# Four S pairs instead of three in each group of the MLP's first product, with the blocks loaded by diagonals

## The chip, the cores and the metric

The kernel runs on one core of a Trainium2 chip. The metric is the device time of one execution, in microseconds (us). Five engines work side by side: TensorE (PE; its weight loads are listed as PEld), VectorE (DVE), ScalarE (ACT), GpSimd (POOL) and SyncE (SP), whose queue issues the loads of weights.

## The reference

A decoder block: attention and a state-space mixer side by side, merged, and then the MLP that this case is about. x has 256 rows of 2048, w_up is 2048 x 8192 and w_down 8192 x 2048, all float32.

```python
merged = sigmoid(gate_att) * (att @ w_att_branch) + sigmoid(gate_ssm) * (y @ w_ssm_branch)
x = x + merged @ w_out
h2 = rms_norm(x, norm2_g)
x = x + square(relu(h2 @ w_up)) @ w_down
```

## The kernel before

Every large product is made in three parts. A float32 weight tile `raw` is copied to a rounded tile `hi` on ScalarE (`split`, L111), and VectorE makes the rest `lo = raw - hi` (L112). The other operand is split in the same way, and TensorE adds hi x hi, hi x lo and lo x hi into one bank of PSUM. Buffers: four `raw` tiles (`RAW`), three `hi` and three `lo`, each of 128 x 1024; a load waits until its `raw` buffer has been read out, a split until TensorE has given a `hi` buffer back.

The MLP goes in two halves of the hidden layer (`for h in range(2)`: `up(h)`, then `down(h)`). `up` has four groups for each half; a group makes 1024 columns of the product for both tiles of 128 rows, over 16 k tiles taken as eight pairs. `down` has two such groups for each half, over 16 pairs each. `mixed` runs a group; the letter of each pair in `UP` or `DOWN` says how its 2 x 2 x 2 block product (two row tiles, two k tiles, two column blocks of 512) is made:

- N and P: eight block products, 24 matmuls of 128x512. The weights are the two `raw` tiles of 1024 columns, each split whole (`pieces_n`).
- S: seven block products of sums of blocks (Strassen's way in Winograd's form), 21 matmuls. `pieces_s` makes the four sums of weight blocks on VectorE: `t13` holds the first and third, `t24` the second and fourth; h1/l1, a hi/lo buffer, h3/l3 and h4/l4 are the splits. h1, l1, t13, t24, h4 and l4 have one buffer each.

The left operands of `up` are made ahead by `norm_task` and `left`, those of `down` by `u_operands` and `left` (L863 to L883), as far as the scheduler moves them forward into the groups of `up`.

A group has seven banks, q1 to q7 in the numbering of `product`. At its end `combine` adds them on VectorE (ScalarE copies q1 first, L1025): `u2 = q6 + q1` and `u3 = q7 + u2` (both L1016), then q2, q5, q3 and q4 with them. Only S pairs write q1, q6 and q7, so these are complete after the last S pair; N pairs write q2, q5, q3 and q4. A next group's product takes a bank as it is given back by `combine`. `u_task` then transposes the results on TensorE (L1073), 16 transposes a group.

The order on each engine is fixed at compile time by a scheduler that lists instructions by the times of its own model; each engine's queue then runs strictly in that order.

Of the kernel before, what the change touches and what calls it, by code (L numbers as in the profile page):

```python
# [32 lines left out]
HD = 128  # L33
IH = 16

UP = "NSNSNSNN"
DOWN = ('NNSNNPPSPPPPSPPP', 'PPSPPPPSPPPPSPPP')
NB = 32
TOPK = 64
# [8 lines left out]
def body(tc, x, x_t, vectors, taps, w_in, dt_bias, a_log, d_skip, bias_t, w_att_branch,  # L48
# [10 lines left out]
    with ctx:  # L59
# [48 lines left out]
        def split(raw, shape):  # L108
            hi = wpool.tile(shape, F32R, name=nm("hi"), tag="hi", bufs=3)
            lo = wpool.tile(shape, F32R, name=nm("lo"), tag="lo", bufs=3)  # L110
            a.copy(hi, raw)  # L111
            v.tensor_tensor(lo, raw, hi.bitcast(F32), op=OP.subtract)  # L112
            return hi, lo
# [831 lines left out]
        def pieces_s(w, kk, c0):  # L945


            r0, r1 = (load(w, kk + i, 1, c0, 1024)[:, 0] for i in range(2))
            h1 = fp.tile([P, 512], F32R, name=nm("h1"), tag="h1", bufs=1)
            l1 = fp.tile([P, 512], F32R, name=nm("l1"), tag="l1", bufs=1)  # L950
            a.copy(h1, r0[:, :512])
            v.tensor_tensor(l1, r0[:, :512], h1.bitcast(F32), op=OP.subtract)
            h2, l2 = (z[:, 0] for z in split(r1, [P, 1, 1024]))
            t13 = fp.tile([P, 2, 512], F32, name=nm("t13"), tag="t13", bufs=1)
            v.tensor_tensor(t13[:, 0], r0[:, :512], r0[:, 512:], op=OP.add)
            v.tensor_tensor(t13[:, 1], r0[:, 512:], r1[:, 512:], op=OP.add)
            h3, l3 = split(t13, [P, 2, 512])
            t24 = fp.tile([P, 2, 512], F32, name=nm("t24"), tag="t24", bufs=1)
            v.tensor_tensor(t24[:, 0], t13[:, 0], r1[:, 512:], op=OP.add)
            v.tensor_tensor(t24[:, 1], t24[:, 0], r1[:, :512], op=OP.add)  # L960
            h4 = fp.tile([P, 2, 512], F32R, name=nm("h4"), tag="h4", bufs=1)
            l4 = fp.tile([P, 2, 512], F32R, name=nm("l4"), tag="l4", bufs=1)
            a.copy(h4, t24)
            v.tensor_tensor(l4, t24, h4.bitcast(F32), op=OP.subtract)
            return {1: (h1, l1), 2: (h2[:, :512], l2[:, :512]), 3: (h2[:, 512:], l2[:, 512:]),
                    5: (h3[:, 0], l3[:, 0]), 7: (h3[:, 1], l3[:, 1]),
                    6: (h4[:, 0], l4[:, 0]), 4: (h4[:, 1], l4[:, 1])}

# [197 lines left out]
```

## Time and profile before

| | us |
|---|---|
| median of 3 runs | 1979.37 (1977.62 to 1980.09) |
| the profiled execution | 1978.39 |
| its span in the trace | 1976.3 |
| PE busy in the span | 1963.7 (99%) |
| DVE busy | 1500.6 (76%) |
| ACT busy | 1063.6 (54%) |

The first product runs from about 1280 to 1458 (first half) and from 1630 to 1802 (second half). A busy time is the union of the instructions' durations; matmuls and VectorE's operations overlap their neighbours, so the cost of one in a row of many is read from start to start. The granted clock of TensorE is 1.0 of full speed in all the stretches below.

### The profile page before, as it was taken

To read this page: it belongs to the slowest core of one execution; us is meant where nothing else is said; L and a number is where in the kernel's file an instruction comes from. 1 tells how busy PE (TensorE), PEld (TensorE's weight loads), DVE (VectorE), ACT (ScalarE), POOL (GpSimd) and SP (SyncE) were. 2 spreads that over 40 slices of the span, in tenths; PEclk is the share of its full clock that TensorE was granted. 3 is DMA by queue.
4 is the path that set the end of the run, shared out by engine and by line. 5 is a ranking of instruction groups with operands and counts; after the bars stand their busy time and mean duration, and the time that the engine had idled before them with its cause. 6 is when DMAs were issued, how large, how long until landed. Compare 5 with 4: busy or idle time off the path is not lost.

```text
span 1976.3 us, 26219 instructions
## 1 busy us (share of the span) xinstructions
PE 1963.7 (99%) x9437; PEld 1633.8 (83%) x9437; DVE 1500.6 (76%) x2465; ACT 1063.6 (54%) x1562; POOL 38.2 (2%) x93
## 2 busy tenths in 40 slices
PE   9999999999999999999999999999999999999998
PEld 7878888888888888888888888788888888888887
DVE  7868656558888887888656556699878888887886
ACT  6555545444455554545544544566665555665554
POOL 2000000000000000000000000000000000000000
PEclk9999999999999999999999999999999999999999
DMA  7646555476666566565566666555565665656664
GB/s 229 211 134 185 182 166 167 160 222 187 181 186 186 181 187 187 176 186 173 171 197 186 193 193 229 174 192 191 193 198 187 211 200 186 204 186 195 193 222 149
DMA packets 132226, 372.25 MB, mean 188 GB/s; under 512 B 18288, under 2 KB 18928, under 8 KB 131840
## 3 DMA queue, kind: packets, MB, share of 16 engines
q1 hardware_dynamic: 128704, 357.87, 58.1%
q0 software_dynamic: 3248, 12.65, 1.9%
q8 instruction: 74, 1.21, 0.2%
q14 instruction: 56, 0.46, 0.1%
q10 hardware_dynamic: 144, 0.06, 0.0%
HBM read 368.37 MB, written 2.16 MB: 187 GB/s over the span
## 4 chain that ended last, share of the span: by engine, by line
PE 98%; DVE 1%; ACT 1%; DMA 0%; issue 0%; SPq 0%; DVEq 0%; ACTq 0%
PE mb L153 42%; PE mb L981 31%; PE mb L127 10%; PE mb L128 5%; PE ab L981 3%; PE ab L748 1%; PE ab L1073 1%; PE ab L458 1%; PE ab L692 0%; PE ab L767 0%; PE ab L740 0%; PE ab L712 0%; DMA raw<-in_w_in_dram 0%; PE ab L552 0%; PE ab L577 0%; PE ab L573 0%
## 5 line engine op out<-in xcount | busy, mean ns | idle before, releaser
L112 DVE TENSOR_TENSOR lo<-raw,hi 128x1024 fp32r<-128x1024 f32 x628 | 765.5, 1222 | 361.1 <-ACT hi L111 359.3
L111 ACT CAST hi<-raw 128x1024 fp32r<-128x1024 f32 x628 | 658.1, 1052 | 619.5 <-PE mb L153 329.1
L153 PE MATMUL mb<-hi,h_hl 128*128 128x512 f32 x1408 | 444.2, 393 | 0.0
L153 PEld LDWEIGHTS mb<-hi,h_hl 128*128 128x128 f32 x1408 | 263.2, 188 | 57.1 <-issue 3.4
L153 PE MATMUL mb<-lo,h_hl 128*128 128x512 f32 x704 | 278.1, 395 | 0.3 <-DVE lo L112 0.3
L981 PE MATMUL mb<-hi,xa 128*128 128x512 f32 x832 | 261.3, 391 | 2.2 <-DVE xn L924 2.2
L127 PE MATMUL mb<-h_hl,hi 128*128 128x512 f32 x768 | 262.5, 396 | 0.0
L128 PE MATMUL mb<-h_hl,lo 128*128 128x256 f32 x768 | 204.2, 286 | 0.0
L981 PEld LDWEIGHTS mb<-hi,xa 128*128 128x128 f32 x832 | 156.1, 188 | 35.0 <-ACT sq L927 2.6
L127 PEld LDWEIGHTS mb<-h_hl,hi 128*128 128x128 f32 x768 | 141.9, 188 | 30.5 <-issue 1.7
L981 PE MATMUL mb<-lo,xa 128*128 128x512 f32 x416 | 163.5, 393 | 0.0
L153 PE MATMUL mb<-hi,yhl 128*128 128x512 f32 x512 | 157.9, 389 | 0.0
L153 PEld LDWEIGHTS mb<-lo,h_hl 128*128 128x128 f32 x704 | 132.3, 188 | 29.1 <-issue 1.3
L981 PE MATMUL mb<-lo,ah 128*128 128x512 f32 x376 | 146.7, 391 | 0.0
L981 PE MATMUL mb<-hi,al 128*128 128x512 f32 x376 | 146.1, 389 | 0.0
L128 PEld LDWEIGHTS mb<-h_hl,lo 128*128 128x128 f32 x768 | 141.3, 189 | 5.3 <-issue 1.7
L981 PE MATMUL mb<-hi,ah 128*128 128x512 f32 x376 | 122.1, 390 | 0.0
L153 PEld LDWEIGHTS mb<-hi,yhl 128*128 128x128 f32 x512 | 96.1, 188 | 19.9
L153 PE MATMUL mb<-lo,yhl 128*128 128x512 f32 x256 | 99.6, 389 | 0.0
L981 PEld LDWEIGHTS mb<-lo,xa 128*128 128x128 f32 x416 | 78.2, 188 | 16.3 <-DVE lo L112 0.4
L981 PEld LDWEIGHTS mb<-lo,ah 128*128 128x128 f32 x376 | 70.6, 188 | 15.0 <-DVE lo L112 0.4
L981 PEld LDWEIGHTS mb<-hi,al 128*128 128x128 f32 x376 | 70.6, 188 | 14.4
(289 smaller groups left out, 2644.8 us busy)
## 6 DMA issues: line engine op xcount, KB each, us to landing
raw<-in_w_in_dram SPq DMA_DIRECT2D x286, 512.0 KB, 3.6
raw<-in_w_up_dram SPq DMA_DIRECT2D x128, 512.0 KB, 4.2
raw<-in_w_down_dram SPq DMA_DIRECT2D x128, 512.0 KB, 4.7
raw<-in_w_ssm_branch_dram SPq DMA_DIRECT2D x64, 512.0 KB, 4.4
raw<-in_w_att_branch_dram SPq DMA_DIRECT2D x32, 512.0 KB, 3.8
raw<-in_w_out_dram SPq DMA_DIRECT2D x32, 512.0 KB, 4.6
abc<-acum_d POOLq DMA_DIRECT2D x16, 512.0 KB, 5.2
bt<-in_bias_t_dram POOLq DMA_DIRECT2D x8, 256.0 KB, 3.1
```

The costliest lines, as they stand in the source:

```text
L111: a.copy(hi, raw)
L112: v.tensor_tensor(lo, raw, hi.bitcast(F32), op=OP.subtract)
L127: pe.matmul(banks[j], hi[:, js], mv, start=kk == 0, stop=False)
L128: pe.matmul(banks[j][:, :S], lo[:, js], mv[:, :S], start=False, stop=kk == nk - 1)
L153: pe.matmul(banks[t][c], st[:, x_ + t * P:x_ + (t + 1) * P], w_[:, c * 512:(c + 1) * 512], start=kk == 0 and i == 0 and not started, stop= ...
L458: pe.matmul(bs[i][:, ds], qiT[rs_, hp, ts], kiT[rs_, ks], start=True, stop=True)
L748: pe.matmul(yd[:, i * 64:(i + 1) * 64], M[:, i], xk[c][:, i * 64:(i + 1) * 64], start=True, stop=True)
L981: pe.matmul(q[i], st, mv, start=left_of[i] == total[i] and n == 0, stop=left_of[i] == 1 and n == 2)
L1073: pe.transpose(b[:, j * S + t * P:j * S + (t + 1) * P], cs[t][c][:, f0:f0 + P], ident)
```

## The change

The seventh of the eight pairs of `up` goes by seven block products, so that pairs two, four, six and seven are S pairs. In `pieces_s`, for both products of the MLP, the two tiles of a pair are no longer two k tiles of 1024 columns: the first, `ra`, holds the upper left and the lower right block of 512, the second, `rb_`, the upper right and the lower left one. Then both sums of `t13` are one operation of 1024 columns, which reads the first block of `rb_` twice. `ra` is split whole; h1 and l1 come from the second block of `rb_`. The names of the pieces follow.

```diff
--- before.py
+++ after.py
@@ -33,7 +33,7 @@
 HD = 128
 IH = 16
 
-UP = "NSNSNSNN"
+UP = "NSNSNSSN"
 DOWN = ('NNSNNPPSPPPPSPPP', 'PPSPPPPSPPPPSPPP')
 NB = 32
 TOPK = 64
@@ -945,24 +945,30 @@
         def pieces_s(w, kk, c0):
 
 
-            r0, r1 = (load(w, kk + i, 1, c0, 1024)[:, 0] for i in range(2))
+            at = w[kk * P:(kk + 1) * P, c0:c0 + 512]
+            W = at.ap[0][0]
+
+            ra, rb_ = (wpool.tile([P, 2, 512], F32, name=nm("raw"), tag="raw", bufs=RAW)
+                       for _ in range(2))
+            for r, o, d in ((ra, 0, P * W + 512), (rb_, 512, P * W - 512)):
+                nc.sync.dma_start(r, bass.AP(tensor=at.tensor, offset=at.offset + o,
+                                             ap=[[W, P], [d, 2], [1, 512]]))
+            h2, l2 = split(ra, [P, 2, 512])
+            t13 = fp.tile([P, 2, 512], F32, name=nm("t13"), tag="t13", bufs=1)
+            v.tensor_tensor(t13, ra, rb_[:, 0].unsqueeze(1).to_broadcast([P, 2, 512]), op=OP.add)
             h1 = fp.tile([P, 512], F32R, name=nm("h1"), tag="h1", bufs=1)
             l1 = fp.tile([P, 512], F32R, name=nm("l1"), tag="l1", bufs=1)
-            a.copy(h1, r0[:, :512])
-            v.tensor_tensor(l1, r0[:, :512], h1.bitcast(F32), op=OP.subtract)
-            h2, l2 = (z[:, 0] for z in split(r1, [P, 1, 1024]))
-            t13 = fp.tile([P, 2, 512], F32, name=nm("t13"), tag="t13", bufs=1)
-            v.tensor_tensor(t13[:, 0], r0[:, :512], r0[:, 512:], op=OP.add)
-            v.tensor_tensor(t13[:, 1], r0[:, 512:], r1[:, 512:], op=OP.add)
+            a.copy(h1, rb_[:, 1])
+            v.tensor_tensor(l1, rb_[:, 1], h1.bitcast(F32), op=OP.subtract)
             h3, l3 = split(t13, [P, 2, 512])
             t24 = fp.tile([P, 2, 512], F32, name=nm("t24"), tag="t24", bufs=1)
-            v.tensor_tensor(t24[:, 0], t13[:, 0], r1[:, 512:], op=OP.add)
-            v.tensor_tensor(t24[:, 1], t24[:, 0], r1[:, :512], op=OP.add)
+            v.tensor_tensor(t24[:, 0], t13[:, 0], ra[:, 1], op=OP.add)
+            v.tensor_tensor(t24[:, 1], t24[:, 0], rb_[:, 1], op=OP.add)
             h4 = fp.tile([P, 2, 512], F32R, name=nm("h4"), tag="h4", bufs=1)
             l4 = fp.tile([P, 2, 512], F32R, name=nm("l4"), tag="l4", bufs=1)
             a.copy(h4, t24)
             v.tensor_tensor(l4, t24, h4.bitcast(F32), op=OP.subtract)
-            return {1: (h1, l1), 2: (h2[:, :512], l2[:, :512]), 3: (h2[:, 512:], l2[:, 512:]),
+            return {1: (h2[:, 0], l2[:, 0]), 2: (h1, l1), 3: (h2[:, 1], l2[:, 1]),
                     5: (h3[:, 0], l3[:, 0]), 7: (h3[:, 1], l3[:, 1]),
                     6: (h4[:, 0], l4[:, 0]), 4: (h4[:, 1], l4[:, 1])}
```

The program has 8932 rows on TensorE where it had 8956, and as many loads as before.

VectorE, where the second group of the first half ends and the third begins. In the kernel before, raw_12326 and raw_12332 are the tiles of the seventh pair (N), raw_12362 and raw_12368 those of the last pair (N), raw_12421 and raw_12427 those of the next group's first pair (N), raw_12471 and raw_12473 those of its second pair (S):

```order
L112 TENSOR_TENSOR lo_12329<-raw_12326,hi_12328 128x1024 [waits DMAHW1_49,Activation_49]
L112 TENSOR_TENSOR lo_12335<-raw_12332,hi_12334 128x1024 [waits DMAHW2_49,Activation_49]
L1016 TENSOR_TENSOR ev_12404<-mb_12043,ev_12402 128x512 [waits PE_49]
L112 TENSOR_TENSOR lo_12365<-raw_12362,hi_12364 128x1024 [waits DMAHW3_49,Activation_49]
L1016 TENSOR_TENSOR ev_12406<-mb_12044,ev_12404 128x512 [waits DVE_49]
L112 TENSOR_TENSOR lo_12371<-raw_12368,hi_12370 128x1024 [waits DMAHW4_49,Activation_49]
L955 TENSOR_TENSOR t_2429_12483<-raw_12471 128x512 [waits DMAHW7_49]
L952 TENSOR_TENSOR l_2426_12476<-raw_12471,h_2425_12475 128x512 [waits Activation_49]
L112 TENSOR_TENSOR lo_12424<-raw_12421,hi_12423 128x1024 [waits DMAHW5_49,Activation_49]
L956 TENSOR_TENSOR t_2429_12483<-raw_12471,raw_12473 128x512 [waits DMAHW0_49]
L959 TENSOR_TENSOR t_2432_12490<-t_2429_12483,raw_12473 128x512 [waits DVE_49]
L112 TENSOR_TENSOR lo_12430<-raw_12427,hi_12429 128x1024 [waits DMAHW6_49,Activation_49]
```

The same place in the changed kernel; the tiles of the last pair are raw_12380 and raw_12386, those of the next group's first pair raw_12439 and raw_12445, those of its second pair raw_12489 and raw_12490; L1034 is the sum of q2, L1022 are u2, u3 and q5 - u2:

```order
L112 TENSOR_TENSOR lo_12383<-raw_12380,hi_12382 128x1024 [waits DMAHW3_49,PE_49,Activation_49]
L112 TENSOR_TENSOR lo_12389<-raw_12386,hi_12388 128x1024 [waits DMAHW4_49,Activation_49]
L970 TENSOR_TENSOR l_2405_12356<-t_2403_12352,h_2404_12355 128x1024 [waits Activation_49]
L112 TENSOR_TENSOR lo_12442<-raw_12439,hi_12441 128x1024 [waits DMAHW5_49,Activation_49]
L1034 TENSOR_TENSOR c_12416<-mb_12056,ev_12420 128x512 [waits PE_49]
L958 TENSOR_TENSOR t_2439_12497<-raw_12489,raw_12490 128x1024 [waits DMAHW7_49,DMAHW0_49]
L1022 TENSOR_TENSOR ev_12422<-mb_12054,ev_12420 128x512 [waits PE_49]
L962 TENSOR_TENSOR l_2441_12500<-raw_12490,h_2440_12499 128x512 [waits Activation_49]
L965 TENSOR_TENSOR t_2444_12507<-t_2439_12497,raw_12489 128x512 [waits DVE_49]
L1022 TENSOR_TENSOR ev_12424<-mb_12055,ev_12422 128x512 [waits DVE_49]
L1022 TENSOR_TENSOR ev_12427<-mb_12057,ev_12422 128x512
L112 TENSOR_TENSOR lo_12448<-raw_12445,hi_12447 128x1024 [waits DMAHW6_49,Activation_49]
```

The merged sum (L958), which waits for two loads, now stands ahead of u2 and u3 and of the next N tile's lo; before, u2 and u3 stood ahead of the first of the half-sums.

TensorE in the second group of the first half, the last S pair and the first products after it. In the kernel before (hi_12328 is of the N pair that follows):

```order
L981 MATMUL mb_12046<-hi_12294,xa_11622 128x512 [waits Activation_49]
L981 MATMUL mb_12044<-hi_12294,xa_11622 128x512
L981 MATMUL mb_12043<-h_2386_12301,xa_11622 128x512 [waits Activation_49]
L981 MATMUL mb_12048<-h_2386_12301,xa_11622 128x512
L981 MATMUL mb_12046<-lo_12295,xa_11622 128x512 [waits DVE_49]
L981 MATMUL mb_12046<-hi_12294,xa_11622 128x512
L981 MATMUL mb_12044<-lo_12295,xa_11622 128x512
L981 MATMUL mb_12044<-hi_12294,xa_11622 128x512
L981 MATMUL mb_12045<-hi_12328,xa_11622 128x512 [waits Activation_49]
L981 MATMUL mb_12046<-hi_12328,xa_11622 128x512
L981 MATMUL mb_12047<-hi_12328,xa_11622 128x512
L981 MATMUL mb_12043<-l_2387_12302,xa_11622 128x512 [waits DVE_49]
```

The same place in the changed kernel, the second of the two adjacent S pairs (h_2399_12344, hi_12348 and h_2404_12355 are its pieces, hi_12382 is of the last N pair):

```order
L987 MATMUL mb_12057<-hi_12348,xa_11622 128x512 [waits Activation_49]
L987 MATMUL mb_12055<-hi_12348,xa_11622 128x512
L987 MATMUL mb_12056<-l_2400_12345,xa_11622 128x512 [waits DVE_49]
L987 MATMUL mb_12056<-h_2399_12344,xa_11622 128x512
L987 MATMUL mb_12056<-hi_12382,xa_11622 128x512 [waits Activation_49]
L987 MATMUL mb_12058<-hi_12382,xa_11622 128x512
L987 MATMUL mb_12057<-lo_12349,xa_11622 128x512 [waits DVE_49]
L987 MATMUL mb_12057<-hi_12348,xa_11622 128x512
L987 MATMUL mb_12055<-lo_12349,xa_11622 128x512
L987 MATMUL mb_12055<-hi_12348,xa_11622 128x512
L987 MATMUL mb_12057<-hi_12382,xa_11622 128x512
L987 MATMUL mb_12054<-h_2404_12355,xa_11622 128x512 [waits Activation_49]
```

The pair behind the last S pair is now the group's last, and the products of the S pair's last piece (h_2404_12355) are put among those of that pair.

## Rows read from the trace of the kernel before

**Rows 1.** The page's first part (busy time, share, instructions of each engine) and the first line of its part on the chain that ended last.

```profile
PE 1963.7 (99%) x9437; PEld 1633.8 (83%) x9437; DVE 1500.6 (76%) x2465; ACT 1063.6 (54%) x1562; POOL 38.2 (2%) x93
...
PE 98%; DVE 1%; ACT 1%; DMA 0%; issue 0%; SPq 0%; DVEq 0%; ACTq 0%
```

**Rows 2.** The timeline of TensorE in the second group of the first half: start, duration, line, operands, count of merged instructions. L1073 are the transposes of u_task.

```profile
1334.51 1.30 PE L981 MATMUL mb<-hi,xa 128*128 128x512 f32 x5
1335.65 0.39 PE L981 MATMUL mb<-h,xa 128*128 128x512 f32 x1
...
1337.46 1.30 PE L981 MATMUL mb<-hi,xa 128*128 128x512 f32 x5
1338.60 0.60 PE L1073 MATMUL ab<-ident,c 128*128 128x128 f32 x4
1338.95 0.48 PE L981 MATMUL mb<-l,xa 128*128 128x512 f32 x1
1339.27 0.40 PE L981 MATMUL mb<-h,xa 128*128 128x512 f32 x1
```

**Rows 3.** The timeline of ScalarE in the second half: the copies of bank q1 at the end of the four groups.

```profile
1648.87 0.59 ACT L1025 COPY ev<-mb 128x512 f32<-128x512 f32 x1 [1.44 <-PE mb L981]
...
1691.82 0.59 ACT L1025 COPY ev<-mb 128x512 f32<-128x512 f32 x1 [0.31 <-PE mb L981]
...
1736.21 0.58 ACT L1025 COPY ev<-mb 128x512 f32<-128x512 f32 x1
...
1779.59 0.57 ACT L1025 COPY ev<-mb 128x512 f32<-128x512 f32 x1
```

**Rows 4.** The view by windows: the first group of the first half in two parts, its second and third group, and the third group of the second half. Columns: the stretch, its length, then busy time (and instructions) of PE, PEld, DVE, ACT and POOL, granted clock, share of the DMA engines, GB/s.

```profile
1280.00:1306.00 26.00, 25.70 (x120) 21.03 (x121) 24.61 (x48) 19.12 (x35) 0.00 (x0) 1.00 0.49 152
1306.00:1330.00 24.00, 24.00 (x109) 19.77 (x107) 21.82 (x30) 14.19 (x18) 0.00 (x0) 1.00 0.67 221
1330.00:1373.50 43.50, 43.50 (x201) 35.98 (x200) 38.67 (x52) 27.16 (x35) 0.00 (x0) 1.00 0.60 193
1373.50:1416.70 43.20, 43.20 (x198) 35.21 (x197) 35.82 (x43) 25.84 (x31) 0.00 (x0) 1.00 0.60 195
...
1717.00:1760.60 43.60, 43.60 (x201) 36.01 (x200) 35.73 (x43) 26.08 (x31) 0.00 (x0) 1.00 0.60 194
```

**Rows 5.** The timeline of VectorE: the third S pair of the third group, first half.

```profile
1387.51 0.69 DVE L952 TENSOR_TENSOR l<-raw,h 128x512 fp32r<-128x512 f32 x1 [2.09 <-ACT h L951]
1388.12 0.68 DVE L955 TENSOR_TENSOR t<-raw 128x512 f32<-128x512 f32 x1
1388.72 0.68 DVE L956 TENSOR_TENSOR t<-raw,raw 128x512 f32<-128x512 f32 x1
1389.33 0.68 DVE L959 TENSOR_TENSOR t<-t,raw 128x512 f32<-128x512 f32 x1
1389.93 1.22 DVE L112 TENSOR_TENSOR lo<-raw,hi 128x1024 fp32r<-128x1024 f32 x1
1391.06 0.68 DVE L960 TENSOR_TENSOR t<-t,raw 128x512 f32<-128x512 f32 x1
1391.66 2.35 DVE L112 TENSOR_TENSOR lo<-raw,hi 128x1024 fp32r<-128x1024 f32 x2
1393.93 1.22 DVE L964 TENSOR_TENSOR l<-t,h 128x1024 fp32r<-128x1024 f32 x1
1395.07 1.22 DVE L112 TENSOR_TENSOR lo<-t,hi 128x1024 fp32r<-128x1024 f32 x1
```

**Rows 6.** The timeline of VectorE in the second group, first half: operations of 256 and of 128 columns of `left`, each with the start of the next operation.

```profile
1346.62 0.42 DVE L883 TENSOR_TENSOR al<-d,ah 128x256 fp32r<-128x256 f32 x1
1346.95 0.68 DVE L959 TENSOR_TENSOR t<-t,raw 128x512 f32<-128x512 f32 x1
...
1351.10 0.28 DVE L870 TENSOR_TENSOR d<-d,u 128x128 f32<-128x128 f32 x1
1351.30 1.22 DVE L112 TENSOR_TENSOR lo<-t,hi 128x1024 fp32r<-128x1024 f32 x1
```

**Rows 7.** The view of waits from 1330 to 1460: who waited for whom, us in total, times, the longest.

```profile
ACT hi L111 <- PE mb L981: 20.6, 18, 2.6
ACT h L951 <- DMA raw<-in_w_up_dram: 13.1, 5, 3.7
...
PEld mb L981 <- DVE lo L112: 0.4, 1, 0.4
```

**Rows 8.** The view of the DMA queues from 60 to 200 us (loads of `wide`, rows of 4 KB) and from 500 to 700 us (mostly loads of `gemm_t` and z, rows of 2 KB): the load queue's packets, MB and share of the 16 engines.

```profile
q1 hardware_dynamic: 6573, 23.98, 55.8%
...
q1 hardware_dynamic: 16807, 32.39, 53.7%
```

**Rows 9.** The timeline of VectorE at the end of the third group, first half (two lo of the last N pair, then the first half-sum of the next group's first S pair), and, from the view of the tile raw from 1330 to 1460, the time from a load's issue to its landing.

```profile
1401.71 1.22 DVE L112 TENSOR_TENSOR lo<-raw,hi 128x1024 fp32r<-128x1024 f32 x1 [0.40 <-ACT hi L111]
1404.43 1.23 DVE L112 TENSOR_TENSOR lo<-raw,hi 128x1024 fp32r<-128x1024 f32 x1 [1.50 <-ACT hi L111]
1407.37 0.69 DVE L955 TENSOR_TENSOR t<-raw 128x512 f32<-128x512 f32 x1 [1.72 <-DMA raw<-in_w_up_dram]
...
DMA to landing us min/median/max: 3.5/4.4/5.4
```

## The prediction

> **What bounds the kernel now.** I read the page's first part, then the windows of the MLP's first product, the pace of single instructions in them, the waits, and last the loads. TensorE is busy 99% of the span and carries 98% of the chain that ended last [rows 1]; what shortens its queue shortens the kernel, as long as its operands are there. A "group" below is one of the eight blocks of 1024 columns of w_up (four in each half of the hidden layer), with eight pairs of k tiles; an S pair goes by seven block products, an N pair by eight. Five matmuls of 128x512 start 1.14 us apart in all (1334.51 to 1335.65), so one takes 0.228; four transposes and one matmul take 0.67 (1338.60 to 1339.27), so a transpose takes 0.11 [rows 2]. A group of five N and three S pairs is 5 x 24 + 3 x 21 = 183 matmuls and 16 transposes, 41.7 + 1.8 = 43.5 us. The copies of the first bank in the second half lie (1779.59 - 1648.87) / 3 = 43.6 apart [rows 3]. So TensorE does not wait there now.
>
> VectorE is the next in line: 38.67 of 43.5 us and 35.82 of 43.2 in groups two and three of the first half, 35.73 of 43.6 in the third of the second half [rows 4]. From start to start 512 columns take 0.60 and 1024 take 1.14 (1388.12 to 1388.72; 1389.93 to 1391.06) [rows 5], 256 take 0.33 and 128 take 0.20 [rows 6]. In groups two to four ScalarE waits 20.6 us for TensorE to give back a hi buffer, that is, the splits run ahead as far as the three buffers let them, and TensorE's own wait for a lo is 0.4 [rows 7].
>
> **The change part by part.**
>
> *One more S pair.* Three matmuls fewer in each of eight groups: 24 x 0.228 = 5.5 us off TensorE, none added. The group becomes 180 matmuls and 16 transposes, 42.8 us. This is the whole of the possible gain. Before the first group the new S pair also gives its left operands two more small subtractions and other copies; they are on VectorE and ScalarE, which at most costs the first group some of its lead.
>
> *VectorE's bill.* An S pair before: five operations of 512 and three of 1024, 3.0 + 3.4 = 6.4 us. After, two sums being one: three of 512 and four of 1024, 1.8 + 4.6 = 6.4 (0.06 less). An N pair: two of 1024, 2.3. The combination: seven of 512, 4.2. A group before: 3 x 6.4 + 5 x 2.3 + 4.2 = 34.9; after: 4 x 6.4 + 4 x 2.3 + 4.2 = 39.0, of 42.8. The second group of each half also does early splits for the second product (3.6 us in the new order, by the paces of [rows 5, 6]): 42.6 of 42.8. What hid VectorE so far is some 8 us of slack a group; four are left, and in two groups none.
>
> The trace shows the merged sum as saving 2 x 0.60 - 1.14 = 0.06 us [rows 5]. [...]
>
> *The diagonal loads.* 512 KB as before, in rows of 2 KB where they were 4 KB. In a stretch that loads by 4 KB rows the queue moves 23.98 MB in 140 us at 55.8% (307 GB/s if it were full), in one with mostly 2 KB rows 32.39 MB in 200 us at 53.7% (302) [rows 8]. I price the shorter rows at nothing; the DMA engines have 40% to spare. What they do cost: the merged sum needs both tiles of a pair, where the first half-sum needed one. A load lands 3.5 to 5.4 us after its issue, 4.4 in the middle [rows 9], and it is issued when its buffer (one of four) is read out.
>
> *Where TensorE would wait.* The place is the boundary of two groups. Call D the end of the last N pair's second lo. It frees the buffer for the next group's first S pair's second tile, which lands at D + 4.4. VectorE's queue from the second group into the third (first half) then is: merged sum, u2, a lo of 512, half of t24, u3, t5, the next lo, 2 x 1.14 + 5 x 0.60 = 5.3, so that lo is ready at D + 9.7. Between its first uses of these two lo tiles TensorE has 31 matmuls and a transpose, 7.2 us. VectorE must be 2.5 ahead at D. Queued behind the sum are u2 and u3, whose banks TensorE needs for the third and fourth product of the next group. In the kernel before the same wait exists (VectorE sat 1.72 us there) [rows 9], but u2 and u3 stand before it, with two N pairs of cover behind the last S pair instead of one.
>
> How far ahead can VectorE be at D? The lo needs a buffer that TensorE gives back 21 matmuls before it uses the lo: 4.8 us, less the cast (1.05), the lo (1.14) and a bank copy ahead of it on ScalarE (0.6): about 2.1 (1.9 after waits of events; I keep 2.1). In the second group, with the early splits, the order sums from one boundary lo to D to 15 x 0.60 + 20 x 1.14 + 6 x 0.33 + 2 x 0.20 = 34.2 us of VectorE against 149 matmuls and 15 transposes, 35.6: if it starts level it is 1.3 ahead, 0.9 with a wait of 0.4 for a hi buffer. In the first group, where VectorE was busy 24.61 + 21.82 of 50 us already [rows 4], I take 0.5 (an estimate between nothing and 2.1).
>
> The sums for the six inner boundaries, needed lead less lead there is. First half: the first one's queue takes 4.4 + 4.6 = 9.0 against 7.6 of TensorE, the second one's 9.7 against 7.2, the third one's 9.7 against 7.4; so 1.4 - 0.5 = 0.9, 2.5 - 0.9 = 1.6 and 2.3 - 2.1 = 0.2. In the second half u2 and u3 stand ahead of the sum, and the queue from D to the next lo is 4.4 + 2.9 = 7.3 or, for the middle one, 8.5, against 5.2 and 7.9: needed 2.1, 0.6, 2.1, so nothing is lost there. Two boundaries lead into the second product, which begins with N pairs, and I put them at nothing. Lost: 2.7 us. Bounds: nothing, if the first tile's arrival governs and all leads are full; 6 x 1.6 = 9.6, if every boundary goes as the worst.
>
> *The adjacent S pairs.* Between the first lo of pair five and that of pair seven VectorE does 5 x 0.60 + 7 x 1.14 = 11.0 us (11.8 with splits in between) against 38 matmuls, 8.6. It loses 2.4 to 3.1 of its lead. Two pairs apart, an N pair paid this back. I count it as met by a lead of 3 built up on the N pair before them; its buffers allow 32 matmuls, 7.3, less 2.2 for cast and lo, 5.1.
>
> *The sum.* -5.5 + 2.7 = -2.8, with some 0.3 for events: -2.5 us. The profiled execution took 1978.39 (span 1976.3 and 2.1 around it), 1.0 under the median of 1979.37; the change is taken from the median: 1976.9. Second product and all before the MLP: the S pairs of w_down load and add in the new way too, under a VectorE with more slack than in the first product; nothing.
>
> **The rivals.** *The cover holds:* VectorE has 4 us of slack a group and TensorE loses under 1.5 in all. For it: TensorE waits for next to nothing now [rows 7], and five of my six boundaries turn on tenths. Against it: the second group's bill. Time: 1979.4 - 5.5 + 0 to 1.5, 1973.9 to 1975.4.
>
> *The second tile governs, slower:* the loads land not at 4.4 but at 5.4, the upper end of the row [rows 9]. Each needed lead grows by 1.0, each lead falls by about 0.4 from the S pairs' own waits inside a group. Boundaries: 2.3 + 3.0 + 1.6 + 1.4 + 1.1 + 1.4 = 10.8, so -5.5 + 10.8 = +5.3, 1984.7. It decides from about 5.2 us on; at 4.4 it does not. Against it: equal rate for both row lengths [rows 8]. [...]
>
> *The change as a saving of matmuls fails:* excluded, the program has 24 fewer.
>
> **How the numbers follow.** A measurement of this kernel can tell 0.2%, 4 us, from no change. Part of the 5.5 given back (1975.4 to 1983.3, likeliest 1976.9): 0.48. Cover holds: 0.36. Slower: 0.16. With rows at both signs of the 4 us mark, the range goes from the full gain, 1973.6 (with 0.3 for the spread of runs), to 1983.0, which leaves most of the slower rival out.
>
> **What would show it.** The copies of the first bank 42.8 apart: cover holds; near 43.2 on average: my sum. By the changed kernel's line numbers: TensorE's weight loads and matmuls at L987 waiting for lo (L112), l4 (L970) or for u2 (L1022) at the ends of groups one and two of the first half, 0.9 and 1.6 us: the boundary step is right. The merged sum (L958) idle before its DMA in most groups for about 1 us or more: the wait is where I put it. VectorE near 39 of 42.8 in a group: its bill is right. Wrong would be: waits of TensorE spread over the S pairs themselves (then the adjacency is the cost), or landing times of the diagonal loads away from 4.4.

## The result and the profile after

| | us |
|---|---|
| before, median of 4 runs | 1979.55 (1977.62 to 1980.09) |
| after, median of 4 runs | 1992.13 (1988.86 to 1993.63) |
| ratio | 1.0064 [1.0052, 1.0076] |
| the profiled execution after | 1993.63, span 1991.6 |

The changed kernel is slower by 0.64%, 12.6 us: on the other side of no change than the forecast, and above its range.

The page's first part and the first line of its chain that ended last, after (to be read against [rows 1]):

```profile
PE 1969.0 (99%) x9413; PEld 1629.0 (82%) x9413; DVE 1528.1 (77%) x2472; ACT 1075.4 (54%) x1579; POOL 38.3 (2%) x93
...
PE 84%; DVE 8%; DMA 4%; issue 2%; ACT 1%; SPq 0%; DVEq 0%; ACTq 0%
```

24 matmuls fewer are there, and TensorE is busy for longer. 14% of the chain has left TensorE, for VectorE, the loads and the gaps of issue. Where in the program, the timeline of TensorE tells: a pass of the first product begins with its first matmul with an operand `xa`, and the second product with the first matmul with `ah` behind the last one with `xa`. (In the changed order one matmul with `ah` stands ahead of that, at 1458.55 and at 1809.22; it is 0.2 us of each pass below.) After (the second and the fourth row begin the second product; the third begins the second half):

```profile
1281.03 0.76 PE L987 MATMUL mb<-hi,xa 128*128 128x512 f32 x1 [2.17 <-DVE xn L924]
...
1461.04 0.39 PE L987 MATMUL mb<-lo,ah 128*128 128x512 f32 x1
...
1633.46 0.84 PE L987 MATMUL mb<-hi,xa 128*128 128x512 f32 x3
...
1811.26 0.39 PE L987 MATMUL mb<-lo,ah 128*128 128x512 f32 x1
```

So a pass of the first product takes 1461.0 - 1281.0 = 180.0 us and 1811.3 - 1633.5 = 177.8, together 357.8. Read in the same way, it took 174.5 and 171.8 before, 346.3. 24 matmuls fewer make 340.8 due: TensorE lost **17.0 us** in the first product, and 352.8 - 349.7 = 3.1 in the second. The rest of the span's 15.3 is 0.7 before the MLP, where TensorE does the same.

The copies of bank q1 in the second half, after, the answer to [rows 3]:

```profile
1666.67 0.59 ACT L1031 COPY ev<-mb 128x512 f32<-128x512 f32 x1 [0.33 <-PE mb L987]
...
1711.43 0.58 ACT L1031 COPY ev<-mb 128x512 f32<-128x512 f32 x1
...
1759.88 0.59 ACT L1031 COPY ev<-mb 128x512 f32<-128x512 f32 x1 [1.39 <-PE mb L987]
...
1802.62 0.59 ACT L1031 COPY ev<-mb 128x512 f32<-128x512 f32 x1 [1.39 <-PE mb L987]
```

They lie 44.8, 48.5 and 42.7 apart. One group runs at the 42.8 that 180 matmuls and 16 transposes give; one is 5.7 late. That one is the boundary behind the second group of the second half, which the prediction had put at nothing. VectorE there:

```profile
1717.72 1.23 DVE L112 TENSOR_TENSOR lo<-raw,hi 128x1024 fp32r<-128x1024 f32 x1 [0.67 <-ACT hi L111]
1718.86 0.68 DVE L1034 TENSOR_TENSOR c<-mb,ev 128x512 f32<-128x512 f32 x1
1719.46 2.00 DVE L1022 TENSOR_TENSOR ev<-mb,ev 128x512 f32<-128x512 f32 x3
1723.80 1.23 DVE L958 TENSOR_TENSOR t<-raw,raw 128x1024 f32<-128x1024 f32 x1 [2.33 <-DMA raw<-in_w_up_dram]
1724.94 0.68 DVE L1037 TENSOR_TENSOR c<-mb,ev 128x512 f32<-128x512 f32 x1
```

and TensorE, with the window that holds its clock:

```profile
1725.77 0.47 PE L987 MATMUL mb<-hi,xa 128*128 128x512 f32 x1 [1.48 <-DVE c L1037]
1727.37 0.50 PE L987 MATMUL mb<-hi,xa 128*128 128x512 f32 x1 [1.13 <-ACT hi L111]
1728.00 0.74 PE L987 MATMUL mb<-lo,xa 128*128 128x512 f32 x1
1728.54 0.63 PE L987 MATMUL mb<-hi,xa 128*128 128x512 f32 x1
1728.97 0.63 PE L987 MATMUL mb<-lo,xa 128*128 128x512 f32 x1
...
1731.52 0.40 PE L987 MATMUL mb<-h,xa 128*128 128x512 f32 x1
```

```profile
1724.00:1732.00 8.00, 5.26 (x15) 3.52 (x14) 8.00 (x10) 4.53 (x7) 0.00 (x0) 0.79 0.28 76
```

Read them in this order. VectorE stands idle 2.33 us for the merged sum's second load. Behind the sum waits L1037, which gives back q5; TensorE waits 1.48 us for it, then 1.13 for a hi. From 1728.5 to 1731.5 matmuls start 0.43 apart, not 0.228: the granted clock is 0.50 there, against 1.00 from 1716 to 1728, and 0.79 in the mean of the 8 us. Behind its waits TensorE so lost another 1.7 us (0.21 x 8); that the waits brought the lower clock about is not shown. The load that all this waits for was the last of four that the queue issued from 1712.96 to 1715.79, after none since 1707.2 (the issues, and the time to landing of the last one):

```profile
1712.96 1.43 SPq L120 DMA_DIRECT2D raw<-in_w_up_dram  x2
1714.66 1.51 SPq L954 DMA_DIRECT2D raw<-in_w_up_dram  x2
...
DMA to landing us min/median/max: 8.0/8.0/8.0
```

It took 8.0 us to land, where the loads of [rows 9] took 3.5 to 5.4.

That is one place. VectorE as a whole, by windows inside the two passes, first before, then after:

```profile
1285.00:1455.00 170.00, 170.00 (x779) 139.67 (x778) 145.94 (x189) 105.25 (x134) 0.00 (x0) 1.00 0.60 194
1640.00:1800.00 160.00, 160.00 (x729) 132.25 (x729) 133.18 (x158) 94.64 (x112) 0.00 (x0) 1.00 0.61 196
```

```profile
1285.00:1455.00 170.00, 166.33 (x750) 133.64 (x749) 156.32 (x197) 111.42 (x143) 0.00 (x0) 1.00 0.57 184
1640.00:1800.00 160.00, 156.37 (x694) 126.17 (x694) 144.87 (x164) 98.59 (x119) 0.00 (x0) 0.99 0.60 191
```

and its waits after, from 1285 to 1455, with those of TensorE in the same stretch:

```profile
DVE t L958 <- DMA raw<-in_w_up_dram: 8.3, 7, 2.1
DVE lo L112 <- ACT hi L111: 4.5, 5, 1.3
...
PEld mb L987 <- DVE lo L112: 3.8, 5, 1.5
PEld mb L987 <- DVE ev L1022: 2.2, 4, 0.6
PE mb L987 <- DVE lo L112: 2.1, 3, 1.0
```

VectorE's 156.3 busy and 8.3 + 4.5 waiting are 169.1 of 170. Before, its longest wait in this stretch was for a hi:

```profile
DVE lo L112 <- ACT hi L111: 11.7, 11, 1.9
```

while ScalarE waited for TensorE to give back a hi buffer [rows 7], which is being ahead. Now most of VectorE's idle time is for late loads, and TensorE waits for lo. These waits are not spread evenly over the pass. The three waits in the last row above, those of its matmuls (PE), stand some 5 us behind the start of the second, the third and the fourth group:

```profile
1331.30 0.50 PE L987 MATMUL mb<-lo,xa 128*128 128x512 f32 x1 [1.02 <-DVE lo L112]
...
1377.28 0.50 PE L987 MATMUL mb<-lo,xa 128*128 128x512 f32 x1 [0.53 <-DVE lo L112]
...
1421.66 0.50 PE L987 MATMUL mb<-lo,xa 128*128 128x512 f32 x1 [0.54 <-DVE lo L112]
```

The time that TensorE lost can be counted from the starts of its instructions: what an interval has over the 0.228 us of a 512-column matmul or the 0.11 of a transpose, where that is more than 0.09. Over the two passes this comes to 17.3 us, and 9.8 of it lie in the first 30 matmuls (7 us) behind the six inner boundaries: 1.3, 1.8 and 1.6 in the first half, 0, 5.1 (1.7 of it clock) and 0 in the second. Another 1.6 is clock at the start of the MLP, and 3.3 lie from the 121st matmul of a group on, where pairs six to eight are. The second tile of the merged sum at the six boundaries landed 5.2, 5.2, 5.1, 3.8, 8.0 and 3.5 us after its issue: TensorE lost time where it landed late, and none where it landed early. (In the second half u2 and u3 stand ahead of the sum as well, so the landing is not the only difference between these boundaries.)

### The profile page after: what moved, and what is told of

The parts are those of the page before. It is cut to its first block, busy times and chain, and to the rows that moved or that the text cites. A ratio compares the mean times of both kernels' runs of the same rounds, so it can differ in the third digit from the quotient of the medians.

```text
span 1991.6 us, 26210 instructions
## 1 busy us (share of the span) xinstructions
PE 1969.0 (99%) x9413; PEld 1629.0 (82%) x9413; DVE 1528.1 (77%) x2472; ACT 1075.4 (54%) x1579; POOL 38.3 (2%) x93
## 4 chain that ended last, share of the span: by engine, by line
PE 84%; DVE 8%; DMA 4%; issue 2%; ACT 1%; SPq 0%; DVEq 0%; ACTq 0%
PE mb L153 42%; PE mb L987 19%; PE mb L127 10%; PE mb L128 5%; DVE lo L112 3%; DMA raw<-in_w_up_dram 3%; PE ab L987 2%; PE ab L748 1%; DMA raw<-in_w_down_dram 1%; DVE t L958 1%; DVE t L965 1%; PE ab L458 1%; DVE t L966 1%; DVE l L962 0%; PE ab L1079 0%
## 5 line engine op out<-in xcount | busy, mean ns | idle before, releaser
L112 DVE TENSOR_TENSOR lo<-raw,hi 128x1024 fp32r<-128x1024 f32 x620 | 755.1, 1222 | 332.5 <-ACT hi L111 331.2
L111 ACT CAST hi<-raw 128x1024 fp32r<-128x1024 f32 x620 | 649.7, 1051 | 584.2 <-PE mb L153 328.7
L987 PE MATMUL mb<-hi,xa 128*128 128x512 f32 x768 | 256.8, 395 | 5.7 <-DVE xn L924 2.2
L987 PEld LDWEIGHTS mb<-hi,xa 128*128 128x128 f32 x768 | 145.2, 190 | 39.6 <-ACT hi L111 5.1
L987 PE MATMUL mb<-lo,xa 128*128 128x512 f32 x384 | 153.8, 401 | 3.2 <-DVE lo L112 3.0
L987 PEld LDWEIGHTS mb<-lo,xa 128*128 128x128 f32 x384 | 73.0, 190 | 21.5 <-DVE lo L112 7.0
L958 DVE TENSOR_TENSOR t<-raw,raw 128x1024 f32<-128x1024 f32 x44 | 53.8, 1224 | 46.0 <-DMA raw<-in_w_down_dram 25.2
```

The source lines that it names most:

```text
L958: v.tensor_tensor(t13, ra, rb_[:, 0].unsqueeze(1).to_broadcast([P, 2, 512]), op=OP.add)
L987: pe.matmul(q[i], st, mv, start=left_of[i] == total[i] and n == 0, stop=left_of[i] == 1 and n == 2)
```

## The experiments

Three theories stood against one another. The boundary: the merged sum, which waits for two loads, stands ahead of the combination and holds up what is behind it. The neighbours: two S pairs side by side take more lead and load buffers than there are. The bill: VectorE has too much to do, wherever it stands. All were measured beside the kernel before on the same chip. "First" is the two passes of the first product together, "second" what follows each of them, the last to the end of the span, both read as above in the profiled execution. "Clock" is what TensorE lost in the first product at the lower clock: in windows of 4 us, the sum of (1 - granted clock) x 4. Two profiled executions of the same code differ by up to some 2.6 us in a product (e14 and after in the first one, where their order is the same; 1.7 of it is clock), so a difference of 1 or 2 us between rows shows nothing. The medians decide. An edit also lets the scheduler order the instructions anew. Apart from e14, whose first product keeps the order of the changed kernel, a row shows its edit together with its order.

| kernel | median | ratio to before | first | clock | second |
|---|---|---|---|---|---|
| before | 1979.55 | | 346.3 | 0 | 349.7 |
| after | 1992.13 | 1.0064 [1.0052, 1.0076] | 357.8 | 3.4 | 352.8 |
| e1_three_new | 1982.62 | 1.0016 [1.0007, 1.0025] | 347.1 | 0 | 352.4 |
| e2_four_old | 1984.75 | 1.0026 [1.0016, 1.0036] | 352.1 | 0 | 349.4 |
| e6_sum_behind_q5 | 1986.73 | 1.0037 [1.0024, 1.0049] | 351.9 | 1.7 | 351.3 |
| e7_cover | 1998.22 | 1.0090 [1.0075, 1.0105] | 366.6 | 1.7 | 351.6 |
| e4_raw5 | 1985.15 | 1.0033 [1.0020, 1.0046] | 349.2 | 1.7 | 353.7 |
| e6r_raw5_behind | 1989.69 | 1.0057 [1.0044, 1.0069] | 354.0 | 1.7 | 355.0 |
| e8_old_raw5_behind | 1981.44 | 1.0008 [0.9999, 1.0017] | 348.6 | 1.7 | 351.4 |
| e9_before_raw5 | 1980.46 | 1.0004 [0.9996, 1.0013] | 347.5 | 1.7 | 351.1 |
| e10_no_l4 | 1982.75 | 1.0018 [1.0009, 1.0026] | 348.7 | 1.7 | 352.2 |
| e11_raw5_no_l4 | 1980.10 | 1.0001 [0.9992, 1.0010] | 344.5 | 0 | 351.8 |
| e3_apart | 1986.70 | 1.0033 [1.0020, 1.0046] | 352.2 | 0 | 351.3 |
| e12_pool_l4 | 2025.82 | 1.0233 [1.0219, 1.0247] | 373.8 | 5.1 | 369.0 |
| e13_l4_twice | 1991.27 | 1.0060 [1.0047, 1.0073] | 355.2 | 1.7 | 351.9 |
| e14_down_old | 1990.24 | 1.0054 [1.0041, 1.0068] | 355.2 | 1.7 | 351.0 |

**The two parts alone.** e1: the changed kernel with three S pairs. e2: the kernel before with four.

```diff
-UP = "NSNSNSSN"
+UP = "NSNSNSNN"
```

```diff
-UP = "NSNSNSNN"
+UP = "NSNSNSSN"
```

> Three S pairs a group as before, with the new loads and the merged sum. TensorE's work is that of before. If the diagonal loads or the merged sum cost by themselves wherever an S pair stands, this is slower than before by a good part of the 12.6 us (36 of the 44 S pairs remain: about +10, 1989). If they only cost where the merged sum stands ahead of u2 and u3 at a group's end, this order (u2 and u3 ahead of it) loses little: within 2 us of before, 1978 to 1981. If the fourth S pair's work on VectorE is the cause, it also equals before.

> Four S pairs (NSNSNSSN) with the old loads and the two half-sums. If the fourth pair in that place is the cause (half-sums again ahead of u2 and u3, adjacent S pairs), this is as slow as the changed kernel, 1988 to 1994, or slower by the saved 0.06 us of each S pair. If the diagonal loads and the merged sum are the cause, it keeps TensorE's saving: 1974 to 1977.

Neither part alone does it: +0.16% and +0.26%, 2.9 and 5.1 us in the medians, each between its two forecasts. With old loads and half-sums the fourth S pair already loses 352.1 - 340.8 = 11.3 us of TensorE and returns more than the 5.5 it saves. The new loads cost a first product with three S pairs next to nothing (347.1 against 346.3), one with four another 5.7 (3.4 of them in the clock column). In the medians the two parts come to 8.0 of the 12.6 us: they make one another worse.

**The boundary.** e6 puts the merged sum of a group's first S pair behind the q5 sum of the combination before it. e7 leaves two N pairs behind the last S pair.

```diff
+            behind = tc.issue_after(q5_done[0]) if q5_done[0] else contextlib.nullcontext()
+            with behind:
-            v.tensor_tensor(t13, ra, ...)
+                v.tensor_tensor(t13, ra, ...)
...
-                v.tensor_tensor(out_[1][1], q[5], u3, op=OP.subtract)
+                q5_done[0] = v.tensor_tensor(out_[1][1], q[5], u3, op=OP.subtract).ins
```

```diff
-UP = "NSNSNSSN"
+UP = "NSSNSSNN"
```

> The changed kernel, with the first merged sum of a group put behind the sum of q5 of the group before, so that u2, u3 and the banks no longer queue behind its wait for two tiles. If that wait at the group's end is the cause, most of the loss in the first product goes: about 16 us of TensorE's waits there fall to 3 to 6, 1978 to 1983. If adjacent S pairs or VectorE's sum of work is the cause, it stays at 1988 to 1994.

> Four S pairs as NSSNSSNN: the same work on every engine, but two N pairs behind the last S pair, and two neighbouring S pairs twice instead of once. If the missing cover at the group's end is the cause: 1974 to 1979. If neighbouring S pairs are the cause, slower than the changed kernel: 1994 to 2004. If VectorE's sum of work is the cause, as the changed kernel: 1988 to 1994.

e6 gives 5.4 us back, between its two forecasts: the sum ahead of the combination is a part. e7 was my remedy for the boundary and made it 6 us worse. The cover itself works: behind the six inner boundaries TensorE loses 0.1 us, where the changed kernel loses 9.8. But twice two S pairs side by side cost more than that, inside the groups. Its waits from 1325 to 1470, the timeline of ScalarE and VectorE in front of an N pair behind two S pairs, and the landing of its loads (issue to landing, 1325 to 1460; after it is 3.4/4.4/6.1, to be read against [rows 9]):

```profile
ACT hi L111 <- DMA raw<-in_w_up_dram: 11.3, 7, 3.9
...
PEld mb L987 <- ACT hi L111: 7.4, 13, 1.6
```

```profile
1411.54 1.05 ACT L111 CAST hi<-raw 128x1024 fp32r<-128x1024 f32 x1 [3.91 <-DMA raw<-in_w_up_dram]
...
1412.62 1.22 DVE L112 TENSOR_TENSOR lo<-raw,hi 128x1024 fp32r<-128x1024 f32 x1 [2.19 <-ACT hi L111]
```

```profile
DMA to landing us min/median/max: 3.6/4.5/7.2
```

An S pair reads each of its two tiles in four operations, on two engines, before the buffer is free. Two such pairs hold all four `raw` buffers, the load of the next N pair is issued late, and the cast, the lo and TensorE follow. The queue's own waits from 1325 to 1470 show it, e7 first, then after: L120 issues the loads of N pairs, L965 is the last operation that reads the first tile of an S pair.

```profile
SPq L120 <- DVE t L965: 50.8, 9, 7.2
```

```profile
SPq L120 <- DVE t L965: 22.4, 4, 6.4
```

Once issued, the loads are not slower in the middle (4.5); the slowest takes 7.2.

**The buffers.** e4: a fifth `raw` buffer in the changed kernel (its space comes from putting the last pair's left operands elsewhere). e9: the same in the kernel before. e6r: e4 with the merged sum and l1 behind q5. e8: as e6r, with the old loads and half-sums.

```diff
-RAW = 4
+RAW = 5
...
+        xa_in = [0, 0, 0, 0, 1, 1, 1, 0]
+        xa_at[7] = 26
...
-                z = XA[g][:, xa_at[j]:xa_at[j] + (7 if UP[j] == "S" else 6)]
+                z = XA[xa_in[j]][:, xa_at[j]:xa_at[j] + (7 if UP[j] == "S" else 6)]
```

> The changed kernel with five raw buffers instead of four in the whole program (room made by putting the last pair's left operands into unused space of the first tile of them). Loads are issued one tile earlier. If what binds neighbouring S pairs and the group's end is the wait for a tile whose buffer was held by an S pair, most of the 12.6 us goes: 1976 to 1982. If VectorE's sum of work is the cause, it stays at 1988 to 1994.

> The kernel before with five raw buffers, to tell what the fifth buffer is worth by itself. TensorE waits for next to nothing there, so 1978 to 1980, unless the stages before the MLP gain from it too, which every run with five buffers would then share.

> The changed kernel with five raw buffers and the first merged sum and l1 of a group behind the sum of q5 of the group before. If late tiles and the order at the group's end are the two causes, both go: 1974 to 1978, TensorE's full saving less 1 to 3. If VectorE's work is the cause: 1985 or more, no better than the order alone gave.

> Four S pairs with the old loads and half-sums, five raw buffers, the first half-sums and l1 of a group behind the sum of q5. Against the run with four S pairs and old loads (1984.7). If late tiles and order are the cause, 1973 to 1977, and 2 us or so under the same with the new loads, since the second product keeps its old pace. If VectorE's work is: 1983 to 1986.

The fifth buffer gives 7.0 us back in the changed kernel (1985.2, between its two forecasts) and nothing in the kernel before: the four S pairs need it, the three don't. Behind the inner boundaries 3.5 us are left of the 9.8. e6r is a miss: both remedies together are worse than the buffer alone. The waits of 1.60 and 1.75 us at the starts of its second product are not the reason, since e4 has 1.73 and 1.52 there; 4.8 us of the difference lie in the first product (354.0 against 349.2), and why is not settled. e8 has both remedies and the old sums. Between its two forecasts, it only comes back to the kernel before: 348.6, 7.8 over 340.8.

**No neighbours.** e3: S pairs at places 0, 2, 4 and 6.

```diff
-UP = "NSNSNSSN"
+UP = "SNSNSNSN"
```

> The changed kernel with its four S pairs of a group at places 0, 2, 4 and 6 (SNSNSNSN in place of NSNSNSSN): as many matmuls, loads and sums, no two S pairs side by side, an S pair right behind the combination in seven of eight groups. If two S pairs side by side, which hold all four load buffers, are most of the loss, the two passes come to about 350, as with a fifth buffer (349.2), and the time to 1983 to 1986. If the merged sum at the combination is most of it, it stands now at every inner end of a group with no pair of two-product kind ahead of it, and the time is 1992 to 2000.

5.4 us better than the changed kernel, although each inner boundary now has an S pair right behind it. So two neighbours cost more than an S pair right behind a boundary does. The boundaries are not free, though: 6.0 us are lost behind the six.

**VectorE's bill.** e10 and e11 leave out l4 (and use l3 in its place) in the changed kernel, and in e4. e13 is the kernel before with l4 written twice, and nothing else.

```diff
-            v.tensor_tensor(l4, t24, h4.bitcast(F32), op=OP.subtract)
...
-                    6: (h4[:, 0], l4[:, 0]), 4: (h4[:, 1], l4[:, 1])}
+                    6: (h4[:, 0], l3[:, 0]), 4: (h4[:, 1], l3[:, 1])}
```

```diff
             v.tensor_tensor(l4, t24, h4.bitcast(F32), op=OP.subtract)
+            v.tensor_tensor(l4, t24, h4.bitcast(F32), op=OP.subtract)
```

> The changed kernel without the fourth pieces' low half: L970, the 1024-element subtraction l4 of every pair of seven products, is left out, and the products 6 and 4 take l3 in its place (the computation is changed there; matmuls, loads, buffers and every other operation stay). VectorE does 1.14 us less for each of the four S pairs of a group, 4.6 of its some 39 us. If VectorE's bill is what the first product waits for, its two passes (357.8 us together in the changed kernel) come down to 345 to 350 and the time to about 1980 to 1985. If the late tiles and the order at the ends of the groups are the cause, whatever VectorE's share, the passes stay at 355 to 358 and the time at 1990 or above.

> The same leaving out (l4 not made, l3 in its place in products 6 and 4) on the changed kernel with a fifth load buffer, whose two passes of the first product take 349.2 us, 8.4 over the 340.8 that 24 matmuls fewer would give. If what is left there is VectorE's bill (158 of 170 us busy), the passes come to 341 to 344 and the time to 1976 to 1979. If it is the merged sum that waits for both tiles and stands ahead of the combination, that does not depend on l4: 347 to 350 and 1983 to 1985.

> The kernel before with the subtraction l4 of every S pair written twice: three S pairs a group as before, no load, order or matmul changed, and VectorE does 3 x 1.22 = 3.7 us more a group of its 43.5, nearly the 4.1 us that the fourth S pair adds. If VectorE's bill alone makes TensorE wait, the two passes of the first product (346.3 us) grow by some 5 to 9 and the time to 1986 or above. If the bill costs only together with two S pairs side by side and the merged sum at the end of a group, they stay within 2 us and the time at 1979 to 1983 (the S pairs of the second product get the operation too, nine of them a half).

The windows of e10, then of e13, in the stretches shown above:

```profile
1285.00:1455.00 170.00, 168.26 (x767) 137.39 (x766) 142.67 (x184) 112.01 (x144) 0.00 (x0) 1.00 0.62 192
1640.00:1800.00 160.00, 158.71 (x718) 129.36 (x717) 132.62 (x153) 101.16 (x121) 0.00 (x0) 1.00 0.64 200
```

```profile
1285.00:1455.00 170.00, 168.47 (x761) 135.90 (x761) 156.47 (x199) 103.98 (x133) 0.00 (x0) 1.00 0.59 188
1640.00:1800.00 160.00, 158.63 (x714) 128.77 (x713) 147.69 (x172) 94.36 (x113) 0.00 (x0) 1.00 0.59 191
```

e13 comes nearest to VectorE's bill by itself. Its loads, its matmuls and the places of its S pairs are the old ones. Its order is not, against the expectation (which also has nine S pairs a half in the second product where there are six): the scheduler counts the second l4 too, and the instructions of all three engines in the first product stand in another order than before. VectorE is as busy as in the changed kernel (156.5 of 170), and the first product grows by 8.9 us (7.2 without the clock), the median by 11. Its waits from 1285 to 1455:

```profile
PEld mb L982 <- DVE lo L112: 3.6, 6, 1.0
PE mb L982 <- DVE lo L112: 1.1, 3, 0.5
...
PEld mb L982 <- DVE l L965: 0.4, 1, 0.4
```

The second writing also makes l4 itself later, but TensorE's wait for it is 0.4; it waits for the lo tiles queued behind. Three of its five longest waits for a lo (at 1305.6, 1355.7 and 1702.1) end 16, 34 and 29 us of VectorE's work without a gap of 0.1, as a backlog would; that the new order has no part in the loss is not shown. The place also differs from the changed kernel's: e13 loses nothing behind the inner boundaries and, apart from the clock, all of it inside the groups. e10 is the reverse: VectorE's bill a little below that of the kernel before (142.7), 9.4 us back in the median, and 348.7 - 340.8 - 1.7 = 6.2 us still lost with VectorE no busier than before, 3.9 of it behind the inner boundaries. With the fifth buffer too (e11) 3.7 are left, and a kernel with every matmul saved, no l4 and five buffers is level with the kernel before (between its two forecasts).

**GpSimd for l4.** e12: e8 with l4 on GpSimd.

```diff
-            v.tensor_tensor(l4, t24, h4.bitcast(F32), op=OP.subtract)
+            nc.gpsimd.tensor_tensor(l4, t24, h4.bitcast(F32), op=OP.subtract)
```

> The kernel before with four S pairs of old loads and half sums, five load buffers, and the sums and l1 behind the q5 sum of the combination (1981.4 us without more), and l4 subtracted on GpSimd in place of VectorE, which so does 1.14 us less per S pair, there and in the second product. If VectorE's bill is what keeps that version from its 5.5 us, the passes of the first product fall from 348.6 to 341 to 344 and the time to 1974 to 1978, below the kernel before. If GpSimd takes over about three us for it, or holds VectorE up, l4 comes later than the products 6 and 4 want it, and the time is 1981 to 1986.

A miss by 40 us. GpSimd's timeline has two of the subtractions as

```profile
1309.73 8.26 POOL L974 TENSOR_TENSOR l<-t,h 128x1024 fp32r<-128x1024 f32 x1 [9.96 <-ACT h L973]
...
1373.38 2.40 POOL L974 TENSOR_TENSOR l<-t,h 128x1024 fp32r<-128x1024 f32 x1 [5.27 <-ACT h L973]
```

where VectorE takes 1.22; VectorE then waits for t24 to be read out ("DVE t L969 <- POOL l L974", 9.0 us from 1285 to 1455).

**The second product.** e14: the changed kernel, with old loads and half-sums in `down`.

```diff
-                    ws = pieces_s(w, kk, c0)
+                    ws = (pieces_old if w is w_down else pieces_s)(w, kk, c0)
```

> The changed kernel with the second product's S pairs made the old way (4 KB loads, half sums), the first product untouched. If the merged sum of the second product costs it the 3 us that it is longer than before (352.8 against 349.7), the time falls to 1988 to 1990. If the second product is only late because the first one hands over a late VectorE, it stays at 1991 to 1993.

1990.24 against 1992.13: the intervals overlap. That the new loads cost the second product a little is what e1 suggests (352.4 with a first product almost unhurt, against 349.7). In its second pass the changed kernel waits 0.63 and 0.43 us for lo, 98 and 105 us behind the start, and e14 does not; e14 waits 1.53 us near the start of the first pass instead. So e14 does not settle it.

## Why the prediction was wrong

*One more S pair* held: 24 matmuls fewer, and 42.7 us for a group where nothing is late.

*VectorE's bill* held as a number and failed as a conclusion. 39.0 of 42.8, 42.6 with early splits, came out as 156.3 of 170. The step "four are left, and in two groups none" was then priced at nothing outside the boundaries. e13 puts as large a bill in the old kernel at 7.2 us, with what its new order adds. The arithmetic was there to be done [rows 2, 5]: an S pair takes 6.4 us of VectorE against 21 x 0.228 = 4.8 of TensorE, an N pair 2.3 against 5.5. VectorE falls behind in every S pair, and can bring in only the lead that three hi and four raw buffers let it store. An average of 91% says nothing of that.

*The adjacent S pairs* is a step that failed outright: "I count it as met by a lead of 3", a cost of nothing. Its buffers were counted for hi, not for raw, which two S pairs hold altogether. e7 (worse by 6), e3 and e4 (better by 5.4 and 7.0) show a cost. The sign that the text named for it, waits in the S pairs themselves, is there with 3.3 us in pairs six to eight. The larger part of the lost time still shows at the boundaries.

*Where TensorE would wait* was right in the place and far too small: 2.7 us, against 9.8 measured behind the six inner boundaries, 8.1 without the clock. The merged sum does wait for its second tile ahead of u2 and u3 at the third boundary of the first half, as foreseen:

```profile
1416.25 1.23 DVE L958 TENSOR_TENSOR t<-raw,raw 128x1024 f32<-128x1024 f32 x1 [2.09 <-DMA raw<-in_w_up_dram]
1417.39 0.69 DVE L1022 TENSOR_TENSOR ev<-mb,ev 128x512 f32<-128x512 f32 x1
...
1418.13 0.19 PEld L987 LDWEIGHTS mb<-hi,xa 128*128 128x128 f32 x1 [0.41 <-DVE ev L1022]
```

The step that failed here is "lands at D + 4.4". 4.4 is the middle of all loads. This tile was the last of three or four loads issued close together at four of the six boundaries, and landed there after 5.1 to 5.2 us, and after 8.0 at the middle boundary of the second half. That boundary, put at nothing, was the worst. I had also counted the time to the next lo there and not to the bank that L1037 behind the sum gives back. In e14, in the same order, the tile took 6.7 there and TensorE lost 2.3 us, not 5.1. e6 gives back 5.4 us where the term was 2.7.

*The diagonal loads*: their price as short rows, nothing, held in the middle of all landings (4.4, as before). The price of waiting for the second of them did not hold, as said. The rival "the second tile governs, slower" had the sign, and at the boundaries the nearest mechanism and size of the three: it put 10.8 us there with a landing of 5.4, and said that it decides from about 5.2 on. A late landing does not need the shorter rows: in e2, with the old rows of 4 KB, the last of four loads issued from 1364.8 to 1367.7 took 6.2 us. The rival too leaves out what is lost inside the groups, in the second product and by the clock, and its 1984.7 falls short of 1992.1. No run changes the landing alone, so what it is worth by itself stays open.

*The second product at nothing* was off by up to 3 us, cause open. The 0.3 us put in for events was the author's estimate; no run shows it by itself.

In sum, of 17.0 us lost in the first product 3.4 are clock; half of that stands at the start of the MLP, where it also falls in runs that change nothing there. The other 13.6 show for the most part at the boundaries, and the remedies point to too little lead of VectorE there, to buffers held by neighbouring S pairs and to loads that come late in consequence. How they divide is open: the bill (e13) shows 7.2 in another place, e10, with a bill no larger than before, still loses 6.2, and the remedies (9.4, 7.0, 5.4 and 5.4 us) come to more than the loss, which fits that each gives back the same lead but does not show it. Left open too: why e6r is worse than e4, and what keeps e11 3.7 us from 340.8. No version tried is faster than the kernel before.

## What to carry to other kernels

When a change moves work from the engine that bounds to the next one, compare the two engines step by step, not by their averages: a step in which the second engine is slower than the first (an S pair here, 6.4 us of VectorE against 4.8 of TensorE) lives off stored lead, and the buffers say how much can be stored. Count every kind of buffer that such a step holds, and for how many operations. Where a forecast rests on the landing of one particular load, ask how many loads are issued just ahead of it; the middle of all landings (4.4 us here) can miss it by a lot (8.0). And before building the change, write the extra operation twice into the old kernel: one run (e13, slower by 11 us) would have given a warning here.

## What the runs showed of the hardware

**The clock.** TensorE's wait of 2.17 us ahead of its first matmul of the MLP is in the kernel before and after and in e13 alike; behind it the granted clock stayed at 1.00 from 1280 to 1284 in some executions (before, e1, e2, e3, e11) and fell to 0.58 to 0.90 in the mean of these 4 us in others (after, e4, e6, e7, e8, e9, e10, e13, e14), at a cost of 1.7 us by the windows. The windows of the kernel before, then of e13, whose matmuls are the same:

```profile
1280.00:1284.00 4.00, 3.70 (x16) 3.10 (x17) 3.64 (x8) 2.96 (x8) 0.00 (x0) 1.00 0.18 70
```

```profile
1280.00:1284.00 4.00, 3.58 (x11) 2.85 (x12) 3.65 (x8) 2.41 (x7) 0.00 (x0) 0.69 0.20 78
```

So 1.7 us of the difference between two single executions can be the clock alone.

**GpSimd.** The same 1024-column subtraction took 2.40 to 8.26 us on GpSimd in e12 (14 of them from 1285 to 1455), 1.22 on VectorE in the kernel before (L964 in [rows 5]).
